# Loading y of both row groups as single 32 KiB rows, and summing in place on ScalarE, in a log-softmax backward kernel

## The chip, the cores and the metric

One core of one Trainium2 chip. The time is device microseconds of one execution, as the median of several. All runs here are of the fast state (granted clock 1.0).

## The reference

```python
# y, dy: (8, 1024, 8192) float32, so 8192 rows of 8192
softmax_x = np.exp(y)
sum_dy = np.sum(dy, axis=-1, keepdims=True)
return (dy - softmax_x * sum_dy).astype(np.float32)
```

Each element of y and dy is read once and one output element is written: 3 x 268.4 MB = 805.3 MB between HBM and SBUF, with little arithmetic.

## The kernel before

The rows are cut into 32 groups of 256. Each partition holds R = 2 rows of a group side by side, so one group of dy, y or the output is a tile of 128 x 16384 floats, 8.4 MB, with 64 KiB in each partition. SBUF holds two such tiles for dy and the output (x0, x1) and one for y. Two groups make a pair; they are called A and B here. A *run* of bytes below is what a DMA moves into one partition without a break: 64 KiB for both rows, 32 KiB for one. In the packet records each such run is one packet.

```python
def sums(x):
    s_t = stats.tile([P, R], fp32, name="s_t")
    half_t = stats.tile([P, 2], fp32, name="half_t")
    nc.vector.tensor_reduce(out=s_t[:, 0:1], in_=x[:, :D], ..., op=ALU.add, negate=True)   # row 0 on VectorE
    for h in range(2):                                                                     # row 1 on ScalarE
        nc.scalar.activation(copied[:], x[:, D + h * H : D + (h + 1) * H], COPY,
                             accum_out=half_t[:, h : h + 1])        # copied: a PSUM tile nobody reads
    nc.vector.tensor_scalar(out=s_t[:, 1:2], ...)                   # -(half 0 + half 1)
    return s_t
# ...
def compute(x, s_t, r):
    for b, e in PIECES:                      # 2048, 3072 and 3072 columns of row r
        cs = slice(r * D + b, r * D + e)
        nc.scalar.activation(y_t[:, cs], y_t[:, cs], EXP)
        nc.vector.scalar_tensor_tensor(out=x[:, cs], in0=y_t[:, cs], scalar=s_t[:, r : r + 1],
                                       in1=x[:, cs], op0=ALU.mult, op1=ALU.add)

for g in range(0, G, 2):
    load_dy(g, x_ts[0])
    load_y(g, 0, W)                          # y of A: one DMA, 64 KiB runs
    s_t = sums(x_ts[0])
    for r in range(R):
        compute(x_ts[0], s_t, r)
    load_dy(g + 1, x_ts[1])
    s_t = sums(x_ts[1])
    for r in range(R):
        load_y(g + 1, r * D, (r + 1) * D)    # y of B: two DMAs, 32 KiB runs
        compute(x_ts[1], s_t, r)
    for j in range(2):
        nc.sync.dma_start(out=out_v[g + j], in_=x_ts[j][:])
```

All DMAs are issued by SyncE (SP), in program order. SP waits before each until its tile is free or full, and the DMA engines work off what it has queued.

## Time and profile before

| | before |
|---|---|
| time, median | 1867.8 us (3 runs), 1867.5 (6 runs, when measured beside the changed kernel) |
| DMA queue's share of the 16 engines' span | 99.9% |
| bytes over the span | 805 MB, 432 GB/s |
| VectorE (DVE) / ScalarE (ACT) busy | 46% / 37% |
| one pair | about 116.3 us |

The page of the kernel before. In the rows of part 2 a digit is the busy share of one of 40 slices, in tenths; in part 5 the columns after the count are busy us, mean ns of one, and the idle time before the group with what ended it.

```profile
span 1865.9 us, 923 instructions
DVE 859.8 (46%) x256; ACT 698.7 (37%) x321; POOL 0.2 (0%) x4
...
DVE  2907429074290732807328073280632806338063
ACT  2606326063260532605336052360523605236052
...
DMA  9999999999999999999999999999999999999999
GB/s 427 424 430 427 430 447 427 427 431 445 427 427 441 426 437 434 438 431 427 437 438 429 433 428 440 434 431 437 425 438 436 433 436 425 439 433 436 434 428 391
...
q1 hardware_dynamic: 16128, 805.31, 99.9%
...
DMA 64%; DVE 13%; ACT 10%; another core or an unknown queue 9%; issue 1%; SPq 0%; DVEq 0%; ACTq 0%
...
L61 ACT ACTIVATE copied<-x 128x4096 f32<-128x4096 f32 x64 | 229.6, 3587 | 864.9 <-DMA x<-in_dy_dram 863.9
```

DMA is the one row without a gap. The chain of waits (the work that ended last, followed back step by step to what released it) gives DVE 13% and ACT 10% of the span.

The timeline of one pair: start, length, engine, line, operation, and in brackets the idle time before it with what ended it. "x2" joins two instructions; a long SP entry is two issues with a wait between them.

```profile
101.02 0.34 SPq L52 DMA_DIRECT2D x<-in_dy_dram  x1
101.47 0.40 SPq L75 DMA_DIRECT2D y_t<-in_y_dram  x1
120.71 0.33 SPq L52 DMA_DIRECT2D x<-in_dy_dram  x1
139.81 8.69 DVE L57 TENSOR_REDUCE s_t<-x 128x1 f32<-128x8192 f32 x1 [46.71 <-DMA x<-in_dy_dram]
...
159.18 14.32 ACT L80 ACTIVATE y_t<-y_t 128x2048 f32<-128x2048 f32 x6 [11.87 <-DMA y_t<-in_y_dram]
...
170.56 9.25 SPq L75 DMA_DIRECT2D y_t<-in_y_dram  x2
178.54 3.59 ACT L61 ACTIVATE copied<-x 128x4096 f32<-128x4096 f32 x1 [5.04 <-DMA x<-in_dy_dram]
...
179.85 29.85 SPq L102 DMA_DIRECT2D out_dram<-x  x2
...
188.25 7.22 ACT L80 ACTIVATE y_t<-y_t 128x2048 f32<-128x2048 f32 x3 [2.26 <-DVE s_t L64]
```

A's sums are over at 148.6, but A's exps wait until 159.2, when the whole y of A is there. A's arithmetic ends at 179.5, and y row 1 of B is issued then. The y row ahead of it in the queue lands at about 188.2 (B's dy at 178.5, plus 9.7 us of transfer; B's exps begin at once, at 188.25, held a moment longer by the sums). That distance, 8.7 us, is called the *lead* below: how long before the landing of the transfer ahead a DMA is issued.

### The profile page before, as it was taken

How to read it: one execution, taken by the hardware profiler on the slowest of the kernel's cores; microseconds unless marked ns; L12 is line 12 of the kernel's file. 1: busy time of each engine (PE TensorE's matmuls, PEld its weight loads, DVE VectorE, ACT ScalarE, POOL GpSimd, SP SyncE). 2: the span in 40 equal slices, each digit the busy share in tenths (PEclk: the TensorE clock that was granted, in tenths of full speed). 3: DMA queues.
4: the chain of work that ended last, by engine and by line, in shares of the span. 5: the costliest groups of instructions: out<-in, count | busy, mean ns of one | idle time of the engine just before them, and what ended most of it. 6: DMA issues, size and time to landing. Idle time of an engine off the chain costs nothing.

```text
span 1865.9 us, 923 instructions
## 1 busy us (share of the span) xinstructions
DVE 859.8 (46%) x256; ACT 698.7 (37%) x321; POOL 0.2 (0%) x4
## 2 busy tenths in 40 slices
DVE  2907429074290732807328073280632806338063
ACT  2606326063260532605336052360523605236052
POOL 0000000000000000000000000000000000000000
DMA  9999999999999999999999999999999999999999
GB/s 427 424 430 427 430 447 427 427 431 445 427 427 441 426 437 434 438 431 427 437 438 429 433 428 440 434 431 437 425 438 436 433 436 425 439 433 436 434 428 391
DMA packets 16135, 805.37 MB, mean 432 GB/s; under 512 B 1792, under 2 KB 1792, under 8 KB 1792
## 3 DMA queue, kind: packets, MB, share of 16 engines
q1 hardware_dynamic: 16128, 805.31, 99.9%
q14 instruction: 7, 0.06, 0.0%
HBM read 536.87 MB, written 268.44 MB: 432 GB/s over the span
## 4 chain that ended last, share of the span: by engine, by line
DMA 64%; DVE 13%; ACT 10%; another core or an unknown queue 9%; issue 1%; SPq 0%; DVEq 0%; ACTq 0%
DMA x<-in_dy_dram 31%; DMA out_dram<-x 30%; DVE x L81 13%; ACT copied L61 6%; ACT y_t L80 4%; DMA y_t<-in_y_dram 3%; SPq L75 0%; DVEq L128 0%; ACTq L128 0%; SPq L52 0%; ACTq L80 0%; ACTq L61 0%
## 5 line engine op out<-in xcount | busy, mean ns | idle before, releaser
L81 DVE SCALAR_TENSOR_TENSOR x<-y_t,s_t,x 128x3072 f32<-128x3072 f32 (+1 forms) x192 | 579.4, 3059 | 255.7 <-ACT y_t L80 255.7
L57 DVE TENSOR_REDUCE s_t<-x 128x1 f32<-128x8192 f32 x32 | 277.8, 8682 | 722.3 <-DMA x<-in_dy_dram 722.3
L80 ACT ACTIVATE y_t<-y_t 128x3072 f32<-128x3072 f32 (+1 forms) x192 | 460.1, 2466 | 269.4 <-DMA y_t<-in_y_dram 253.2
L61 ACT ACTIVATE copied<-x 128x4096 f32<-128x4096 f32 x64 | 229.6, 3587 | 864.9 <-DMA x<-in_dy_dram 863.9
L61 ACT ACTIVATION_READ_ACCUMULATOR copied<-x 128x1 f32 x64 | 11.9, 186 | 0.0
L64 DVE TENSOR_SCALAR s_t<-half_t 128x1 f32<-128x1 f32 x32 | 6.5, 204 | 0.0
L61 ACT ACT_TABLE_LOAD x1 | 1.3, 1283 | 0.7 <-PEq L117 0.7
L117 POOL MEMSET const-bfloat16-1.0<- 128x1 bf16 x1 | 0.1, 101 | 0.0
L117 POOL MEMSET const-uint8-127<- 128x1 uint8 x1 | 0.1, 101 | 0.0
L117 POOL MEMSET const-float32-0.0<- 128x1 f32 x1 | 0.1, 98 | 0.2 <-issue 0.2
L117 POOL MEMSET const-float32-1.0<- 128x1 f32 x1 | 0.1, 98 | 0.0
## 6 DMA issues: line engine op xcount, KB each, us to landing
y_t<-in_y_dram SPq DMA_DIRECT2D x32, 4096.0 KB, 18.1
x<-in_dy_dram SPq DMA_DIRECT2D x32, 48.3
out_dram<-x SPq DMA_DIRECT2D x32, 32.5
y_t<-in_y_dram SPq DMA_DIRECT2D x16, 57.6
```

What stands on the lines that cost most here:

```text
L57: nc.vector.tensor_reduce(out=s_t[:, 0:1], in_=x[:, :D], axis=mybir.AxisListType.X, op=ALU.add, negate=True)
L61: nc.scalar.activation(copied[:], x[:, D + h * H : D + (h + 1) * H], COPY, accum_out=half_t[:, h : h + 1])
L64: nc.vector.tensor_scalar(out=s_t[:, 1:2], in0=half_t[:, 0:1], scalar1=half_t[:, 1:2], scalar2=-1.0, op0=ALU.add, op1=ALU.mult,)
L80: nc.scalar.activation(y_t[:, cs], y_t[:, cs], EXP)
L81: nc.vector.scalar_tensor_tensor(out=x[:, cs], in0=y_t[:, cs], scalar=s_t[:, r : r + 1], in1=x[:, cs], op0=ALU.mult, op1=ALU.add,)
L117: nc = _bacc.Bacc("TRN2", target_bir_lowering=False, num_devices=1)
```

## The change

Its intent: A can start on row 0 when half of its y is there, and each y row is asked for once the same row of the other group has been used. The sums of row 1 become one ScalarE instruction that writes the copy back onto itself, and PSUM is no longer used.

```diff
-        for h in range(2):
-            nc.scalar.activation(
-                copied[:], x[:, D + h * H : D + (h + 1) * H], COPY, accum_out=half_t[:, h : h + 1]
-            )
+        nc.scalar.activation(x[:, D:], x[:, D:], COPY, accum_out=second_t[:])
 ...
-    def load_y(g, lo, hi):
-        nc.sync.dma_start(out=y_t[:, lo:hi], in_=y_v[g][:, lo:hi])
+    def load_y(g, r):
+        nc.sync.dma_start(out=y_t[:, r * D : (r + 1) * D], in_=y_v[g][:, r * D : (r + 1) * D])
 ...
     for g in range(0, G, 2):
-        load_dy(g, x_ts[0])
-        load_y(g, 0, W)
-        s_t = sums(x_ts[0])
-        for r in range(R):
-            compute(x_ts[0], s_t, r)
-        load_dy(g + 1, x_ts[1])
-        s_t = sums(x_ts[1])
-        for r in range(R):
-            load_y(g + 1, r * D, (r + 1) * D)
-            compute(x_ts[1], s_t, r)
+        for j in range(2):
+            load_dy(g + j, x_ts[j])
+            s_t = sums(x_ts[j])
+            for r in range(R):
+                load_y(g + j, r)
+                compute(x_ts[j], s_t, r)
```

The order of the DMAs is the same as before, except that A's y is two DMAs in place of one.

More of the change, by code (lines that the diff above doesn't have):

```diff
@@ L35 @@
     assert N == G * P * R and D == 8192 and G % 2 == 0
-    H = D // 2
     PIECES = [(0, 2048), (2048, 5120), (5120, D)]
@@ L45 @@
     stats = ctx.enter_context(tc.tile_pool(name="stats", bufs=3))
-    psum = ctx.enter_context(tc.tile_pool(name="psum", bufs=1, space=bass.MemoryType.PSUM))
     x_ts = [pool.tile([P, W], fp32, name=f"x{j}") for j in range(2)]
     y_t = pool.tile([P, W], fp32, name="y_t")
-    copied = psum.tile([P, H], fp32, name="copied")
     def load_dy(g, x):
@@ L55, in sums @@
         s_t = stats.tile([P, R], fp32, name="s_t")
-        half_t = stats.tile([P, 2], fp32, name="half_t")
+        second_t = stats.tile([P, 1], fp32, name="second_t")
         nc.vector.tensor_reduce(
@@ L59, in sums @@
         )
-        for h in range(2):
-            nc.scalar.activation(
-                copied[:], x[:, D + h * H : D + (h + 1) * H], COPY, accum_out=half_t[:, h : h + 1]
-            )
+        nc.scalar.activation(x[:, D:], x[:, D:], COPY, accum_out=second_t[:])
         nc.vector.tensor_scalar(
-            out=s_t[:, 1:2],
-            in0=half_t[:, 0:1],
-            scalar1=half_t[:, 1:2],
-            scalar2=-1.0,
-            op0=ALU.add,
-            op1=ALU.mult,
-        )
-        return s_t
-    def load_y(g, lo, hi):
-        nc.sync.dma_start(out=y_t[:, lo:hi], in_=y_v[g][:, lo:hi])
+            out=s_t[:, 1:2], in0=second_t[:], scalar1=-1.0, scalar2=None, op0=ALU.mult
+        )
+        return s_t
+    def load_y(g, r):
+        nc.sync.dma_start(out=y_t[:, r * D : (r + 1) * D], in_=y_v[g][:, r * D : (r + 1) * D])
     def compute(x, s_t, r):
```

## The prediction

> **What bounds the kernel now.** The DMA engines. The row of slices shows DMA at 90% or more in all 40; the queue table gives queue 1 99.9% of the 16 engines' span: 805.31 MB in 1865.9 us, 432 GB/s. The Trainium skill, "DMA: Bandwidth & Descriptors", section "Where 436 GB/s comes from", puts the ceiling at 435.2 GB/s; the trace agrees to 0.7%. By that figure the bytes need an estimated 1850 us. DVE is busy 46%, ACT 37%.
>
> **How a pair runs** (timeline, 101 to 217 us). A pair is about 116.3 us. dy of group A lands at 139.8, the whole y of A at 159.2, dy of B at 178.5, then y of B in two rows (188.2, 198.0), then both outputs. A's arithmetic starts when all of y is there and ends at 179.5; its store is queued at 179.9. SP queues ahead: B's y rows are issued 8 us and 8.7 us before the transfer ahead of each ends, the second store 7.5 us. In the packet records no DMA engine has a gap over 0.3 us. The chain's DVE 13% and ACT 10% run under full DMA engines.
>
> **What the change does.**
> - Issue order on SP is unchanged except that A's y becomes two DMAs of 4 MB: 48 y loads become 64. Same bytes.
> - A's y row 0 lands about 9.7 us earlier (149.5), just after the sums (148.6). A's row 0 ends near 161, row 1 near 170.7; B's y rows and A's store are issued about 9 us earlier, and only stand longer in the queue. B's half and the second store keep their times.
> - "Load once the row is used" frees nothing for A: when A's y is issued (101.5), the previous pair's arithmetic has been over since 93; what holds the queue is the store of x.
> - In-place sums: two copies of 3587 ns with two accumulator reads of 186 ns become one of each. From the exp lengths (1905 ns at 2048, 2747 at 3072: 0.82 ns per element, 0.22 us fixed) the copy of 8192 should take about 6.95 us; ACT busy falls from 699 to about 686 us. Hidden: DVE's reduce (8.68 us) is longer.
> - Shorter runs: a 64 KiB packet takes 2418 ns (median), a 32 KiB one 1214 median, 1226 mean. Per engine 128 long packets become 256 short ones: +1.3 us by medians, +4 us by means. Against it, most slow 32 KiB packets stand in B's second y row; with earlier issue part of their excess (about 3 us an engine) may go.
>
> On the critical path is therefore only packet cost: +1 to +4 us, minus 0 to 3.
>
> **Prediction.** 1868.5 us, 1864 to 1874 eight times in ten: no change. Faster by over 2%: 1%; within 2%: 97%; slower by over 2%: 2%.
>
> **What would show the steps.** DMA 9 in all slices, about 432 GB/s; 8192 data packets of 64 KiB and 8192 of 32 KiB (about 18,430 packets in all); the first store of a pair issued about 9 us earlier after A's dy lands; pair period 116.2 to 116.6 us; 32 ACT copies of about 6.95 us.
>
> **What would make it wrong.** A slot where the queue runs dry (GB/s dips every 116 us), for example if the in-place copy held back the DVE reduce or the store; 32 KiB runs costing more than 1226 ns when queued back to back; SBUF writes of ACT slowing packets beyond 2418 ns.

## The result

| | before | after |
|---|---|---|
| time, median of 6 | 1867.53 us | 1867.93 us |
| range | 1866.81 to 1868.07 | 1867.63 to 1868.26 |
| ratio after / before | | 1.0002, 95% interval 0.999 to 1.0015 |

A ratio here is the mean time of one kernel's fast runs over that of the other's of the same rounds, so it is not quite the ratio of the medians.

The page of the changed kernel, the same lines as shown of before:

```profile
span 1865.9 us, 890 instructions
DVE 862.1 (46%) x256; ACT 691.1 (37%) x257; POOL 0.2 (0%) x4
...
DVE  4707447074470744707347073460634606356163
ACT  4506335063350634505344053440524405244152
...
DMA  9999999999999999999999999999999999999999
GB/s 424 427 422 433 440 436 429 428 433 440 430 433 429 434 435 437 434 427 432 440 433 431 430 432 438 433 437 427 433 438 437 429 431 431 442 429 434 431 431 396
...
q1 hardware_dynamic: 18432, 805.31, 99.9%
...
DMA 79%; ACT 10%; DVE 6%; another core or an unknown queue 2%; SPq 1%; issue 0%; DVEq 0%; ACTq 0%
...
L56 ACT ACTIVATE x<-x 128x8192 f32<-128x8192 f32 x32 | 224.9, 7030 | 975.5 <-DMA x<-in_dy_dram 975.5
```

The span, the bytes and the DMA share are what they were; the mean period of a pair is 116.2 us (116.3 before). The rows of DVE and ACT have another rhythm (4707 where 2907 stood), and the chain now gives DVE 6% instead of 13%. The time didn't follow.

The timeline of the same pair in the changed kernel:

```profile
101.37 0.34 SPq L48 DMA_DIRECT2D x<-in_dy_dram  x1
101.80 1.77 SPq L63 DMA_DIRECT2D y_t<-in_y_dram  x2
120.79 0.33 SPq L48 DMA_DIRECT2D x<-in_dy_dram  x1
140.44 8.69 DVE L53 TENSOR_REDUCE s_t<-x 128x1 f32<-128x8192 f32 x1 [47.04 <-DMA x<-in_dy_dram]
...
150.19 7.21 ACT L68 ACTIVATE y_t<-y_t 128x2048 f32<-128x2048 f32 x3 [2.63 <-DMA y_t<-in_y_dram]
...
161.56 10.04 SPq L63 DMA_DIRECT2D y_t<-in_y_dram  x2
...
171.66 38.79 SPq L86 DMA_DIRECT2D out_dram<-x  x2
179.20 7.03 ACT L56 ACTIVATE x<-x 128x8192 f32<-128x8192 f32 x1 [12.08 <-DMA x<-in_dy_dram]
...
188.97 7.22 ACT L68 ACTIVATE y_t<-y_t 128x2048 f32<-128x2048 f32 x3 [2.65 <-DMA y_t<-in_y_dram]
```

A's exps begin at 150.2 instead of 159.2. B's y rows and A's store are issued 8 to 9 us earlier (161.6 instead of 170.6; 171.7 instead of 179.9). But dy of B lands at 179.2 (178.5 before) and row 0 of B's y at 189.0 (188.2): the DMA engines were already busy with what stood ahead. B's y row 1 is issued at 171.3, so its lead has grown from 8.7 to 17.6 us.

### The profile page after: what moved, and what is told of

Same layout as the page of the kernel before. It is cut to its first block, busy times and chain, and to the rows that moved or that the text cites. A ratio compares the mean times of both kernels' runs of the same rounds, so it can differ in the third digit from the quotient of the medians.

```text
span 1865.9 us, 890 instructions
## 1 busy us (share of the span) xinstructions
DVE 862.1 (46%) x256; ACT 691.1 (37%) x257; POOL 0.2 (0%) x4
## 3 DMA queue, kind: packets, MB, share of 16 engines
q1 hardware_dynamic: 18432, 805.31, 99.9%
## 4 chain that ended last, share of the span: by engine, by line
DMA 79%; ACT 10%; DVE 6%; another core or an unknown queue 2%; SPq 1%; issue 0%; DVEq 0%; ACTq 0%
DMA y_t<-in_y_dram 42%; DMA out_dram<-x 37%; ACT y_t L68 10%; DVE x L69 6%; SPq L63 0%; SPq L48 0%; DVEq L112 0%; ACTq L112 0%; ACTq L68 0%
## 5 line engine op out<-in xcount | busy, mean ns | idle before, releaser
L56 ACT ACTIVATE x<-x 128x8192 f32<-128x8192 f32 x32 | 224.9, 7030 | 975.5 <-DMA x<-in_dy_dram 975.5
L56 ACT ACTIVATION_READ_ACCUMULATOR x<-x 128x1 f32 x32 | 6.0, 187 | 0.0
L57 DVE TENSOR_SCALAR s_t<-second_t 128x1 f32<-128x1 f32 x32 | 4.6, 144 | 0.0
```

Of the source, the lines that this page charges most:

```text
L56: nc.scalar.activation(x[:, D:], x[:, D:], COPY, accum_out=second_t[:])
L57: nc.vector.tensor_scalar(out=s_t[:, 1:2], in0=second_t[:], scalar1=-1.0, scalar2=None, op0=ALU.mult)
```

## The experiments

Theory: the DMA engines are full from the first transfer to the last, all arithmetic lies under them, and the change only lengthens the lead. Rivals: the change has a gain and a loss that cancel; the chain's shares of DVE and ACT are real time; short runs are expensive.

### e1_split_only: the row loads alone

The kernel before, PSUM sums kept, with

```diff
-        load_y(g, 0, W)
 ...
         for r in range(R):
+            load_y(g, r * D, (r + 1) * D)
             compute(x_ts[0], s_t, r)
```

> The kernel before with one part of the change: y of group A in two rows. Theory (DMA engines full throughout, arithmetic hidden): only packet cost moves, +0 to +2 us on 1867.5, so 1867 to 1870 us, although A's arithmetic ends about 9 us earlier in each pair. Rival (the change has a gain and a loss that cancel): the split is one of the two; if its earlier arithmetic counts, 16 pairs x 9 us = up to 144 us faster; if only its shorter runs count as the mean packet of before has it (+4 us), about 1872 us, with the in-place sums giving 4 us back.

Measured: 1868.11 us against 1867.70 of the kernel before, ratio 1.0004 (0.9991 to 1.0016).

### e2_inplace_only: the in-place sums alone

The kernel before with only the new `sums`.

> The kernel before with only the in-place sums. Theory: 1867 to 1868.5 us, no difference; ACT busy falls by about 13 us, DVE unchanged. Rival (gain and loss cancel): 3 to 4 us faster, about 1864 us.

Measured: 1867.61 us against 1867.70, ratio 1.0002 (0.9989 to 1.0014). ACT busy fell by 9.4 us (698.7 to 689.3), which is less than the 13 expected.

What follows from the two: neither part moves the time, so there are no two effects of 4 us that cancel; both 1872 for e1 and 1864 for e2 lie outside the intervals (1867.7 x 1.0016 = 1870.7, x 0.9989 = 1865.6). Effects of 1 or 2 us are below what these runs resolve.

### e3_y_8k: y in 8 KiB runs

The changed kernel, every row of y as four DMAs:

```diff
-        nc.sync.dma_start(out=y_t[:, r * D : (r + 1) * D], in_=y_v[g][:, r * D : (r + 1) * D])
+        for q in range(4):
+            lo = r * D + q * (D // 4)
+            hi = lo + D // 4
+            nc.sync.dma_start(out=y_t[:, lo:hi], in_=y_v[g][:, lo:hi])
```

> The changed kernel with every y row loaded as four DMAs of 8 KiB runs. Theory: a packet costs 10 ns fixed (2 x 1214 less 2418)[...], so an 8 KiB packet takes 311 ns and a row on an engine 1244 instead of 1214; times 512 rows an engine is +15 us, with completions about +17: 1884 to 1886 us, +0.9%. Rival (shorter runs cost what the means of before say, 16 ns per extra 32 KiB packet, or more because the pipeline stalls): +25 to +50 us, 1893 to 1918 us. If packets cost nothing: 1868.

(The figure for a KiB in this expectation was a slip and is cut. From the medians it is (1214 - 10) / 32 = 37.6 ns, and with it the 311 ns come out.)

Measured: 1882.62 us, ratio to the kernel before 1.008 (1.0067 to 1.0094). That is 14.7 us over the changed kernel's 1867.93, which was timed in another session. The 8 KiB packets took 312 ns (median), as expected; the sum came out a little under the 17 us forecast, and in the records packets overlap (the queue's share is 100.2%; packet time of an engine rose by 20.1 us, the span by 15.2). Taking off 192 more completions of 9 ns (16 packets of 4 bytes end each DMA), each of 1536 extra packets of an engine cost (14.7 - 1.7) us / 1536 = 8.4 ns. The rival's 25 to 50 us is out. For the change itself, with 128 extra packets an engine, that is an estimate of 1.1 us.

### e4_no_arith: the same DMAs without the arithmetic

The changed kernel with every arithmetic instruction cut to 16 columns. The output is wrong: it is nearly dy itself.

```diff
-            cs = slice(r * D + b, r * D + e)
+            cs = slice(r * D + b, r * D + b + 16)
 # and the sums: two tensor_reduce of 16 columns
```

> The changed kernel with every arithmetic instruction cut to 16 columns; wrong result on purpose, all DMAs and their order as in the changed kernel. Theory (bound by DMA bytes alone): 1864 to 1868.5 us, DVE and ACT busy under 5%. Rival (the shares of DVE and ACT in the chain of the changed kernel, 16% together, are time on the critical path): about 1570 us; if a part is, in proportion.

Measured: 1868.63 us, 0.1 over the edge of the forecast; ratio to the kernel before 1.0005 (0.9991 to 1.0018). From its page:

```profile
DVE 41.7 (2%) x256; ACT 28.8 (2%) x193; POOL 0.2 (0%) x4
...
DMA  9999999999999999999999999999999999999999
...
q1 hardware_dynamic: 18432, 805.31, 99.9%
...
DMA 73%; another core or an unknown queue 22%; DVE 1%; ACT 1%; SPq 1%; issue 0%; ACTq 0%; DVEq 0%
```

This is the plainest proof. With 2% of DVE and ACT left, the time is that of the full kernels, and the chain has almost no arithmetic in it. The 16% that the chain of the changed kernel gives to DVE and ACT was never to be had. Nor was the 23% of before: the kernel before moves the same bytes and takes the same time as this run, which has next to no arithmetic.

A warning on correctness: the comparison with the reference called even this run correct. Worked out from the drawn inputs, exp(y) times the sum has a root mean square of 0.018 against 1.0 of dy, so leaving most of it out passes. "Correct" in these runs therefore doesn't show that the arithmetic is right. That the change keeps it right rests on reading the code.

### e5_before_extra13 and e6_after_extra13: the lead put to the test

If the change only lengthens the lead, it should show as room for more work. Both kernels get 13 us of idle VectorE reduces in A between its two rows; nobody reads their result.

```diff
             compute(x_ts[0], s_t, r)
+            if r == 0:                       # in the changed kernel: r == 0 and j == 0
+                for width in (8192, 4096):
+                    extra_t = stats.tile([P, 1], fp32, name="extra_t")
+                    nc.vector.tensor_reduce(out=extra_t[:], in_=x_ts[0][:, :width], axis=..., op=ALU.add)
```

> The kernel before with 13 us of idle DVE work (reduces whose result nobody reads) between the two rows of group A; result stays right. Theory: B's y row 1 is issued 8.7 us before the queue would run dry, so 13 us more is 4.3 us too late, plus about 2 us to get DMA going: 6 us per pair, +100 us (80 to 120), about 1968 us, and DMA busy share visibly below 100%. Rival (DVE time in the chain is critical): +16 x 13 = +209 us. If DVE time is never critical: +0.

> The changed kernel with the same 13 us of idle DVE work at the same place. Theory: the change moved A's arithmetic 9 us earlier, so B's y row 1 is now issued 17.9 us before the queue would run dry, and 13 us fit: 1866 to 1872 us. Rival (the change bought nothing at all): as for the kernel before with the same work, about +100 us; rival (DVE in the chain is critical): +209 us.

Measured: the kernel before with the extra work 1994.15 us, ratio 1.0677 (1.0659 to 1.0694), 126.8 us over its 1867.31. The changed kernel with the same work: 1870.47 us, ratio 1.0026 (1.0001 to 1.0052), with one run of four at 1879.9. The page of the first, then a table of stretches of the same run (window, length, DVE, ACT and POOL busy, clock, DMA share, GB/s; packets count where they start, so a share can pass 1):

```profile
DMA  9898998989989899898998989989899898998989
GB/s 421 358 442 379 421 421 367 433 379 421 421 366 434 379 421 438 360 422 379 421 442 358 430 379 413 441 358 442 368 429 424 367 433 368 431 433 367 421 379 400
...
q1 hardware_dynamic: 16128, 805.31, 94.9%
```

```profile
444.50:448.50 4.00, 4.00 (x2) 3.76 (x2) 0.00 (x0) 1.00 0.00 0
449.00:452.00 3.00, 3.00 (x1) 2.96 (x2) 0.00 (x0) 1.00 0.89 306
```

and SP's issues there:

```profile
448.90 0.33 SPq L75 DMA_DIRECT2D y_t<-in_y_dram  x1
449.27 0.43 SPq L108 DMA_DIRECT2D out_dram<-x  x1
```

Row 0 of B's y had landed at 444.7, row 1 was issued at 448.9: a lead of minus 4.2 us, and for that time no engine moved a byte. The page of the changed kernel with the same work shows no gap:

```profile
DVE 1062.5 (57%) x288; ACT 691.1 (37%) x257; POOL 0.2 (0%) x4
...
DMA  9999999999999999999999999999999999999999
...
q1 hardware_dynamic: 18432, 805.31, 99.9%
```

and B's y row 1 is issued while row 0 of B's y still has 5.4 us to go (it lands at 421.4, and the exps begin):

```profile
416.06 0.33 SPq L63 DMA_DIRECT2D y_t<-in_y_dram  x1
...
421.50 7.22 ACT L68 ACTIVATE y_t<-y_t 128x2048 f32<-128x2048 f32 x3 [2.64 <-DMA y_t<-in_y_dram]
```

The same 200 us or so of DVE work that cost the kernel before 127 us costs the changed kernel 3. So the change did what it was built for; the kernel before just had no shortage for it to end. The expectation for the first was 80 to 120 us, and it lost more. The packet records say why: over the whole run the mean engine stood idle 98.7 us longer than in the kernel before (span less the time of its data packets: 101.9 against 3.2), and slow packets added 28.2 us (the time over the median of their size, 32.6 against 4.4), together 126.9. Per pair that is 6.2 us dry (the 4.2 of lateness and the 2 that were allowed for getting DMA going), and 1.8 of slow packets that I had not counted.

### e7_after_extra22: the limit of the longer lead

As e6, with widths (8192, 8192, 4096).

> The changed kernel with 21.7 us of idle DVE work at that place. Theory: 3.8 us over the slack of 17.9, plus about 2 us to get DMA going: 6 us per pair, +95 us (75 to 120), about 1963 us; that is, like the kernel before with 13 us. Rival (arithmetic of A can take any time): 1868 us.

Measured: 1979.16 us, ratio 1.06 (1.0584 to 1.0616), 111.9 us over the kernel before (75 to 120 expected). The DMA row has 8s again (share 95.6%), and B's y row 1 was issued 3.2 us after the landing ahead. The changed kernel has a limit too; it lies further out.

### e8_both_whole: the opposite change

The kernel before with B's y loaded whole too, so that all runs are 64 KiB.

```diff
+        load_y(g + 1, 0, W)
         for r in range(R):
-            load_y(g + 1, r * D, (r + 1) * D)
             compute(x_ts[1], s_t, r)
```

> The kernel before with y of B also loaded whole in one DMA (all runs 64 KiB). Theory (what counts is that the queue never runs dry, run length next to nothing): it can be issued only when A's arithmetic is over (179.5), 1 us after dy of B has landed (178.5), and B's store comes only after a whole group's arithmetic behind it: 3 us dry at the load and 2 to 4 us at the store, 5 to 7 us per pair, +80 to +120 us. Rival (run length is what counts): 2 to 4 us faster than before, 1864 us.

Measured: 1995.12 us, ratio 1.0683 (1.0667 to 1.0699): 127.8 us slower, somewhat over the forecast, as slow packets were again not counted in it. Each pair has two restarts: B's y and B's store are both issued about 1.0 us after the landing ahead. Idle time (89.8 - 3.2) and slow packets (45.5 - 4.4) make 127.7 us. Its runs are the longer ones, and it lost because SP issued these two DMAs too late. In this kernel the order and time of issue count; 32 or 64 KiB doesn't. Its page also shows what the row of DMA can't tell:

```profile
DMA  9999999999999999999999999999999999999999
...
q1 hardware_dynamic: 13824, 805.31, 95.5%
```

There is a 9 in every slice although the engines are dry twice in each pair, because a digit of 9 means 90% or more. The share and the rate (404 GB/s, where the kernel before has 432) show it.

### e9_after_extra13_again and e10_before_extra6: two more points

e9 is e6 unchanged; e10 is e5 with the single width 6144.

> The changed kernel with 13 us of idle DVE work once more, for the one run of four at 1880 us. Theory (13 us fit into the slack of 17.9): most runs 1867 to 1870 us, an odd run above being scatter of the state of the machine. Rival (a remaining slack of under 5 us is too small for the skew of the 16 engines, so that the queue runs dry now and then): several of the runs between 1870 and 1885 us, and dry spells in the records of the profiled run.

> The kernel before with 6.5 us of idle DVE work in A. Theory: it fits into the 8.7 us of slack, 1867 to 1870 us, although DVE works 104 us more in all. Rival (each microsecond of DVE in the chain costs, and the loss with 13 us was that): half of the +127 us that 13 us cost, about 1931 us.

Measured: e9 1869.43 us (1868.59 to 1870.88), ratio 1.0015 (1.0002 to 1.0027). The run at 1880 didn't come again in five, and the profiled run has no dry spell but at its start and end. I count it as scatter, which isn't shown: that run itself was not profiled. 2.5 us over before remain, and I have no cause for them.

e10: 1906.71 us against 1866.92, ratio 1.022 (1.0206 to 1.0234). **Here my expectation failed.** 6.5 us did not fit into a lead of 8.7; they cost 2.5 us per pair. The rival's 1931 didn't hold either. Stretches around the transfers in one pair of e10:

```profile
424.00:426.00 2.00, 2.00 (x2) 0.90 (x2) 0.00 (x0) 1.00 1.15 426
426.00:428.00 2.00, 2.00 (x1) 0.84 (x1) 0.00 (x0) 1.00 0.89 344
428.00:433.00 5.00, 5.00 (x1) 5.00 (x3) 0.00 (x0) 1.00 0.98 419
433.00:435.00 2.00, 2.00 (x3) 1.37 (x1) 0.00 (x0) 1.00 1.12 295
435.00:437.00 2.00, 2.00 (x2) 0.00 (x0) 0.00 (x0) 1.00 0.81 229
```

B's y row 1 was issued at 424.85, 2.2 us before the row ahead counted as landed. The engines hardly fell idle (11.8 us more than in the kernel before, over the whole run), but the rate fell twice: at the start of the late transfer, where the first 32 KiB packet of an engine took up to 2.2 us instead of 1.2, and again in its last two packets. Over the run slow packets added 27.3 us; with the idle time that is 39.1 of the 39.8 us measured. The 2.5 us are a mean: the lead is 2.2 us in every pair, yet most pairs take in turn about 118 and 120 us, where the kernel before has 116.3. Why is open.

So in this kernel a DMA must be queued well before the one ahead lands. Six leads, each from SP's issue time and the next landing, beside the loss per pair:

| | lead of B's y row 1 | us per pair over the kernel before |
|---|---|---|
| changed kernel | +17.6 us | 0.0 |
| before | +8.7 | 0 |
| e6/e9, after + 13 us | +5.4 | 0.2 |
| e10, before + 6.5 us | +2.2 | 2.5 |
| e7, after + 21.6 us | -3.2 | 7.0 |
| e5, before + 13 us | -4.2 | 7.9 |

(Losses are the differences of the medians, over 16 pairs.) A lead of 5.4 us is all but enough, 2.2 is not. Once the lead is gone, 3.7 us (e5) and 3.8 us (e7) come on top of the lateness, and in e8 about 3 for each of the two late DMAs. Why the last packets of a late transfer are slow too stays open.

## Why the prediction was right

The time is 1867.9 us where 1868.5 was forecast, inside 1864 to 1874. Point by point:

- **The bound: right.** The changed kernel has DMA at 9 in every slice and 432 GB/s. e4 shows it: the same time with 2% of the arithmetic. The ceiling of 435.2 GB/s that the Trainium skill gives ("DMA: Bandwidth & Descriptors", "Where 436 GB/s comes from") fits the runs without a dry spell, at 431 or 432 (428 with the 8 KiB runs of e3). The same section also says that for transfers between HBM and SBUF the HBM side binds at about 358; the 432 measured here on one core is above that, so it doesn't hold. No run here tells what in the DMA path sets the rate. "Perfetto Trace Analysis", "Engine Utilization" (under "Roofline"), gives a practical ceiling of about 120% of 358 GB/s for one core running alone; 432 / 358 = 121% agrees.
- **Where the gain went: right.** A's row 0 began at 150.2 (forecast 149.5), its end let B's y row 0 go at 161.6 (161), row 1 at 171.3 (170.7) and A's store at 171.7 (171). All of it stayed ahead in a queue that was never empty, and the landings came no earlier. e5 and e6 show that the room so made is real, and that nothing used it.
- **"Frees nothing for A": agrees.** A's y is issued 0.4 us after dy of A in both kernels (101.47 and 101.80); the store of the pair before holds the queue until then. No run changed this alone.
- **Packet cost: not resolved.** Forecast +1 to +4 us, less up to 3. Packets were 8192 and 8192 as forecast, 18,432 in the queue. The medians differ by 0.4 us and the interval runs from -1.9 to +2.8 us, so that the forecast came within 0.6 us of the median is in part luck. e3 measured the term by itself, 8.4 ns a packet, so +1.1 us, at the lower end of the forecast. The mean of 1226 ns for a 32 KiB packet, from which the "+4" came, was not a cost of short runs: with twice as many of them the changed kernel has the same median, 1214, and a mean of 1218; the excess is a few slow packets, whose number doesn't grow with the runs. The "minus 0 to 3" was in part there: the excess of the 32 KiB packets fell from 3.1 to 2.1 us an engine (2.1 with the split alone, 2.8 with the sums alone).
- **In-place sums: right in effect, a little off in size.** The copy took 7.03 us (forecast 6.95) and ACT busy fell by 7.6 us, not 13: the longer copies make 2.6 us of the difference, the exps took 1.7 us more in all, and the old accumulator reads had overlapped the copies by 1.3 us more. None of it shows in the time (e2).
- **The lead, which the prediction read as "8 us and 8.7 us before the transfer ahead of each ends": used too generously.** It was enough for this change. But e10 shows that the last few of these microseconds aren't free: the first packet starts 1.0 us after the issue began (424.85 to 425.81), and first packets take up to 1.0 us more than 1.2.

## What to carry to other kernels

When the row of the DMA engines is full in every slice and the bytes over the span stand at the engines' ceiling, earlier arithmetic and longer queues buy nothing, whatever shares the chain of waits gives to the compute engines; cut the arithmetic out once, and the time that remains is the floor for that order of DMAs. The row alone isn't enough: e8 has a 9 in every slice and is 7% slower. What such a change does buy is lead, the time between the issue of a DMA and the end of the one ahead: read it off the timeline before you add work or take away a buffer, and keep some of it; in this kernel about 5 us were needed. Between 32 and 64 KiB, run length was worth under 0.1% (the estimate from e3), while 64 KiB runs asked for too late (e8, two restarts of the queue in each pair) cost 7%.

## What the Trainium skill lacked or had wrong

- "DMA: Bandwidth & Descriptors", "Latency and other measured facts", gives about 0.6 us to the first byte of a DMA issued by SP. This agrees: in e5 the issue ended at 449.23 and the first packet started at 449.87 (0.64 us; it is 0.97 from the issue's start). But no page says that a DMA issued with a lead of 2.2 us on a full queue already costs 2.5 us, nor that one issued into an empty queue costs 3 to 4 us beyond its lateness (e5, e7, e8): about 2 us until the engines are full again, first packets of 1.5 to 2.0 us instead of 1.2, and slow last packets.
- "DMA: Bandwidth & Descriptors", "Why small descriptors are slow", names about 3 cycles of fixed cost per packet and 32 bytes of descriptor metadata, for small descriptors. No page gives a time per packet for long runs: for 8 to 64 KiB the records show about 10 ns per packet (2 x 1214 - 2418), and e3 8.4 ns in the time of the kernel.
- "Perfetto Trace Analysis", "Identifying the Most-Contended Engine", says to judge DMA by its rate and not by occupancy; that held: e8 has a 9 in every slice and 404 GB/s, e10 a share of 99.3% and 423 GB/s. It lacks the counterpart for dependency chains: here the chain gave 23% of the span to DVE and ACT before and 16% after, and with the arithmetic cut out (e4) the time stayed within 0.2% of both.
